# Stick-breaking attention: four steps under way, first steps in the single banks, values gathered into the last step's bank

## The chip, the cores and the metric

The kernel runs on one core of one Trainium2 chip. The metric is the time of one execution in microseconds (us); the median of three runs stands for the kernel. A core has five engines that run their own instruction lists in order and wait for each other through semaphores: TensorE (PE in the rows, with its weight loads as PEld), VectorE (DVE), ScalarE (ACT), GpSimd (POOL) and SyncE (SP, which here only starts transfers). TensorE writes its results into a memory of eight banks; DVE and ACT read them there.

## The reference

Two blocks of a network run one after the other on 512 positions of width 1024. The change lies in the second block's attention, which is all that has to be seen here:

```python
def stick_breaking_attention(q, k, v):
    # beta[t,s] = sigmoid(q_t.k_s / sqrt(Dh)), s < t
    # A[t,s]    = beta[t,s] * prod_{s<j<t} (1 - beta[t,j])
    # o_t       = sum_{s<t} A[t,s] v_s
    ...
        z = jnp.einsum("bqhd,bkhd->bhqk", qb, kb) * scale
        ...
        log_beta = jax.nn.log_sigmoid(z)
        log_one_minus = jnp.where(mask, jax.nn.log_sigmoid(-z), 0.0)
        tail = lax.cumsum(log_one_minus, axis=3, reverse=True) - log_one_minus
        weights = jnp.where(mask, jnp.exp(log_beta + tail), 0.0)
        outs.append(jnp.einsum("bhqk,bkhd->bqhd", weights, vb))
```

There are 8 heads of 64. Around it stand a projection to queries, keys, values and two gates, a causal convolution of 31 taps on the gated part with a layer norm, and an output projection of the attention and the convolution together.

## The kernel before

Everything but the attention is large products: each weight is split into a part in a reduced format and a remainder, and each product is three matmuls (`mm3`, lines 127 to 129). TensorE is the engine that the whole kernel is built around; the others prepare its operands and read its results.

**The stretch of the change.** The heads are taken two at a time: four pairs of heads, `hp` from 0 to 3. The two heads of a pair are `e` = 0 and 1. For a pair the 512 keys are cut into blocks of 128, and these are worked in three steps `n`: step 0 holds key blocks 2 and 3, step 1 block 1, step 2 block 0 (`STEPS`, line 765). A step is 384, 384 or 512 columns wide for each head (`WIDE`). Each step has two halves of work:

- `sticks(hp, n)`: TensorE forms the scores `z` (line 785, 6 or 12 matmuls, then line 790 for the mask). Then softplus is worked out: an absolute value (on ACT at line 794 for the first two pairs, on DVE at line 797 for the last two), exp and log on ACT (lines 799 and 800), `max(z, 0) +` on DVE (line 801), and a split into a high part (a cast on ACT, line 135) and a low part (a subtraction on DVE, line 136). These two parts are the step's block, `blk(hp, n)`.
- `breaks(hp, n)`: TensorE subtracts from `z`, in the same bank, the sums over later keys: with `negone` the blocks of the pair's earlier steps (line 814) and with `negtri` the step's own block (line 817). ACT then takes the exponent (line 819): these are the weights, `taken(hp, n)`. They wait for the step's own chain of six operations, and the matmuls of line 814 also for the blocks of the earlier steps.

After the three steps of a pair, `gather(hp)` multiplies the weights with the values (line 829) and ACT and DVE split the result into `qT` (lines 135 and 136, tile G).

**Banks.** The scores of a step lie in a double bank (`pair()`, tag pp, of which there are three). Two single banks (`ps0`, `ps1`) are left: `project()`, which forms the values before the attention, uses both in turn, `gather` takes `ps0`, and the norm of the convolution (`conv_norm`, line 889) `ps1`. A `pair` or a `single` is free again when its last reader is done.

**Order.** The code is written with the steps of `sticks` up to two ahead of `breaks` (line 979), and the first step of the next pair is not taken ahead while the last one of this pair is open. A scheduler then lays out each engine's list from the code by its own simulation, so the lists below are what counts. In these lists 120 convolution taps on DVE (line 851, tile H, 128x512 each) stand between the attention's operations, and ACT also splits weights for later products (lines 199 and 202). After the attention the same list goes on with `attended(u)`, the output projection of its result (lines 127 to 129 on tile G), parts of which stand already among the last pair's steps; then the same for the convolution's half.

Of the kernel before, what the change touches and what calls it, by code (L numbers as in the profile page):

```python
# [10 lines left out]
F32 = mybir.dt.float32  # L11
# [68 lines left out]
def block_kernel(  # L80
# [694 lines left out]
    def sticks(hp, n):  # L775

        w = WIDE[n]
        zt = pair()
        z = zt[:, :, :w]

        for i, (ks, qs) in enumerate(((kT[0], qT[0]), (kT[0], qT[1]), (kT[1], qT[0]))):
            for a in STEPS[n]:
                for e in range(2):
                    hs = slice(e * HD, (e + 1) * HD)
                    pe.matmul(z[:, e, cols_of(a)], ks[hs, hp, a * P : (a + 1) * P],  # L785
                              qs[hs, hp, a * P :], start=i == 0 and a < 3, stop=False,
                              skip_group_check=True)
        for a in STEPS[n]:
            for e in range(2):
                pe.matmul(z[:, e, cols_of(a)][:, :P], identr, never, start=False, stop=False,  # L790
                          skip_group_check=True)
        ex = v3(t4(), 2, w)
        if hp < 2:
            act.activation(ex, z, AF.Abs)
        else:

            dve.tensor_scalar(ex.bitcast(I32), z.bitcast(I32), 0x7FFFFFFF, None,
                              ALU.bitwise_and)
        act.activation(ex, ex, AF.Exp, scale=-1.0)
        act.activation(ex, ex, AF.Ln, bias=1.0)  # L800
        dve.scalar_tensor_tensor(ex, z, 0.0, ex, ALU.max, ALU.add)
        zs[hp, n] = z
        return copy_split(*blk(hp, n), ex)

    def breaks(hp, n):

        w = WIDE[n]
        z = zs.pop((hp, n))
        for e in range(2):
            for a in STEPS[n]:  # L810
                out = z[:, e, cols_of(a)]
# [7 lines left out]
        return act.activation(taken(hp, n), z, AF.Exp)  # L819

    def gather(hp):

        o = single(0)
# [40 lines left out]
    def place(i):  # L864
        if i not in stk:
            name = ("D0", "B0", "D1", "C0", "C1", "B1", "E1")[i]
            stk[i] = slot(name, F32R if i < 4 else F32)
        return stk[i]

    def blk(hp, n):  # L870

        tl = place((hp % 2, 2, 3)[n])
        return tuple(part(tl, 2, WIDE[n], 2 * WIDE[n] * i) for i in range(2))

    def taken(hp, n):

        at = (0, 1024 * (hp % 2), 768)[n]
        return part(place(6 if n == 1 else 4 + hp % 2), 2, WIDE[n], at)
# [94 lines left out]
    conv(10, sticks(*seq[0]))  # L973
    conv(14, sticks(*seq[1]))
    project()
    todo = 2
    for i, x in enumerate(seq):

        while todo < len(seq) and todo <= i + 2 and not (x[1] == 2 and seq[todo][1] == 1):
            conv(2, sticks(*seq[todo]))  # L980
            todo += 1
        weighted = breaks(*x)
        if x[1] == 2:
            gathered = gather(x[0])
# [131 lines left out]
```

## Time and profile before

| | |
|---|---|
| median of three runs | 1245.53 us (1244.40 to 1246.41) |
| the profiled execution | 1245.94 us |
| span of its instructions | 1244.2 us |
| TensorE busy | 1230.3 us, 99% of the span |
| VectorE, ScalarE busy | 754.0 us (61%), 495.0 us (40%) |
| TensorE's granted clock, mean | 0.995 |

The profile is of one execution; its own time lies 1.74 us above its span and 0.41 us above the median. [...] Times in the rows are microseconds from the span's start; the attention's steps lie between about 752 and 842 us.

### The profile page before, as it was taken

To read this page: it belongs to the slowest core of one execution; us is meant where nothing else is said; L and a number is where in the kernel's file an instruction comes from. 1 tells how busy PE (TensorE), PEld (TensorE's weight loads), DVE (VectorE), ACT (ScalarE), POOL (GpSimd) and SP (SyncE) were. 2 spreads that over 40 slices of the span, in tenths; PEclk is the share of its full clock that TensorE was granted. 3 is DMA by queue.
4 is the path that set the end of the run, shared out by engine and by line. 5 is a ranking of instruction groups with operands and counts; after the bars stand their busy time and mean duration, and the time that the engine had idled before them with its cause. 6 is when DMAs were issued, how large, how long until landed. Compare 5 with 4: busy or idle time off the path is not lost.

```text
span 1244.2 us, 13667 instructions
## 1 busy us (share of the span) xinstructions
PE 1230.3 (99%) x5712; PEld 1014.1 (82%) x5712; DVE 754.0 (61%) x823; ACT 495.0 (40%) x534; POOL 113.5 (9%) x137
## 2 busy tenths in 40 slices
PE   9999999999999999999999999999999999999998
PEld 7889888788888888888888887667888888888887
DVE  7855634744766674466373899877575555346532
ACT  6433424623544342243255338764343333123310
POOL 1100210012000000000053440000400000000000
PEclk9999999999999999999999999899999999999999
DMA  7223222312222222222346254301322222222222
GB/s 274 101 104 132 102 102 68 136 68 98 73 100 102 102 102 102 88 85 99 119 152 169 68 130 104 106 1 68 102 102 82 89 100 102 102 102 102 84 70 83
DMA packets 21597, 126.71 MB, mean 102 GB/s; under 512 B 2336, under 2 KB 4256, under 8 KB 7840
## 3 DMA queue, kind: packets, MB, share of 16 engines
q1 hardware_dynamic: 20096, 117.20, 26.7%
q0 software_dynamic: 1152, 8.39, 3.5%
q8 instruction: 44, 0.72, 0.2%
q10 hardware_dynamic: 288, 0.26, 0.1%
q14 instruction: 17, 0.14, 0.0%
HBM read 115.35 MB, written 2.10 MB: 94 GB/s over the span
## 4 chain that ended last, share of the span: by engine, by line
PE 90%; DVE 4%; POOL 2%; ACT 2%; issue 1%; DMA 1%; SPq 0%; DVEq 0%; POOLq 0%; ACTq 0%
PE pp L129 27%; PE pp L127 27%; PE pp L128 27%; DVE H L851 2%; PE ps L128 1%; PE ps L129 1%; PE ps L127 1%; POOL col L746 1%; PE pp L814 1%; PE pp L817 1%; PE ps L829 1%; DMA wlo<-raw 1%; POOL col L745 1%; PE pp L785 0%; PE ps L326 0%
## 5 line engine op out<-in xcount | busy, mean ns | idle before, releaser
L199 ACT CAST whi<-raw 128x2048 fp32r<-128x2048 f32 (+3 forms) x109 | 197.9, 1817 | 415.5 <-PE pp L128 335.7
L129 PE MATMUL pp<-B,wlo 128*128 128x512 f32 x672 | 262.5, 391 | 0.2
L127 PE MATMUL pp<-B,whi 128*128 128x512 f32 x672 | 261.7, 390 | 0.8 <-ACT whi L199 0.7
L128 PE MATMUL pp<-C,whi 128*128 128x512 f32 x672 | 262.2, 390 | 0.0
L205 DVE TENSOR_TENSOR wlo<-raw,whi 128x2048 fp32r<-128x2048 f32 (+3 forms) x101 | 219.3, 2172 | 66.1 <-ACT whi L199 65.6
L128 PE MATMUL pp<-G,whi 128*128 128x512 f32 x448 | 175.0, 391 | 0.0
L129 PE MATMUL pp<-F,wlo 128*128 128x512 f32 x416 | 162.2, 390 | 0.0
L127 PE MATMUL pp<-F,whi 128*128 128x512 f32 x416 | 161.5, 389 | 0.0
L129 PEld LDWEIGHTS pp<-B,wlo 128*128 128x128 f32 x672 | 126.1, 188 | 28.2 <-DVE wlo L205 1.5
L127 PEld LDWEIGHTS pp<-B,whi 128*128 128x128 f32 x672 | 126.3, 188 | 28.0 <-ACT whi L199 1.7
L128 PEld LDWEIGHTS pp<-C,whi 128*128 128x128 f32 x672 | 126.2, 188 | 26.8 <-issue 0.5
L128 PEld LDWEIGHTS pp<-G,whi 128*128 128x128 f32 x448 | 84.1, 188 | 17.5 <-issue 0.2
L655 DVE SCALAR_TENSOR_TENSOR H<-H,sm,H 128x512 f32<-128x512 f32 x132 | 92.8, 746 | 0.7
L634 DVE TENSOR_TENSOR A<-pp,A 128x1024 f32<-128x1024 f32 x23 | 28.2, 1224 | 105.5 <-PE pp L129 105.5
L129 PEld LDWEIGHTS pp<-F,wlo 128*128 128x128 f32 x416 | 78.1, 188 | 16.5 <-issue 0.2
L127 PEld LDWEIGHTS pp<-F,whi 128*128 128x128 f32 x416 | 78.1, 188 | 16.4 <-issue 0.2
L851 DVE SCALAR_TENSOR_TENSOR H<-H,sm,H 128x512 f32<-128x512 f32 x120 | 83.2, 742 | 2.7 <-ACT H L132 2.5
L660 DVE TENSOR_TENSOR H<-pp,rb 128x1024 f32<-128x1024 f32 x22 | 26.8, 1224 | 50.6 <-PE pp L129 44.4
L132 ACT ACTIVATE H<-H,sm 128x512 f32<-128x512 f32 x70 | 54.3, 808 | 4.6 <-DVE H L707 4.6
L1010 DVE TENSOR_TENSOR H<-pp,rb 128x512 f32<-128x512 f32 x22 | 15.2, 691 | 60.4 <-PE pp L129 55.3
L127 PE MATMUL pp<-D,whi 128*128 128x512 f32 x112 | 43.6, 389 | 0.0
L128 PE MATMUL pp<-E,whi 128*128 128x512 f32 x112 | 43.6, 389 | 0.0
(315 smaller groups left out, 1826.3 us busy)
## 6 DMA issues: line engine op xcount, KB each, us to landing
raw<-in_wts SPq DMA_DIRECT2D x99, 1024.0 KB, 4.8
wlo<-raw POOLq DMA_DIRECT2D x8, 1024.0 KB, 7.0
raw<-in_wts SPq DMA_DIRECT2D x8, 768.0 KB, 4.2
A<-in_xT SPq DMA_DIRECT2D x3, 512.0 KB, 6.7
out<-A SPq DMA_DIRECT2D x3, 512.0 KB, 2.8
D<-in_memT SPq DMA_DIRECT2D x1, 1024.0 KB, 11.4
raw<-in_wts SPq DMA_DIRECT2D x3, 256.0 KB, 7.6
A<-in_xT SPq DMA_DIRECT2D x2, 256.0 KB, 3.9
```

What stands on the lines that cost most here:

```text
L127: pe.matmul(out, wh, xh, start=start, stop=False, **kw)
L128: pe.matmul(out, wh, xl, start=False, stop=False, **kw)
L129: pe.matmul(out, wl, xh, start=False, stop=stop, **kw)
L132: act.activation(out, in_, AF.Identity, scale=scale, bias=bias)
L199: act.copy(hi[:, cs], raw[:, cs])
L205: dve.tensor_tensor(lo[:, cs], raw[:, cs], hi[:, cs].bitcast(F32), ALU.subtract)
L634: dve.tensor_tensor(hu, pt, hu, ALU.add)
L655: dve.scalar_tensor_tensor(dst, hs[:, k : k + 512], w(k), dst, ALU.mult, ALU.add)
L660: dve.tensor_tensor(hs[:, :, 2:], pt, over2(rb), ALU.mult)
L745: pool.tensor_scalar(ms, ms, rr2[:, t : t + 1], EPS, ALU.mult, ALU.add)
L851: tap = dve.scalar_tensor_tensor(cv[:, i, :], cc[:, i, k : k + 512], par("dw_w", 4 * k + i), cv[:, i, :], ALU.mult, ALU.add)
L1010: dve.tensor_tensor(hs[:, 2:514], pt[:, 0, :], rb, ALU.mult)
```

## The change

Three things are altered together.

- **Where the scores of a step lie.** Step 0 of every pair of heads now takes the two single banks, one for each head; steps 1 and 2 take a double bank as before. So three double banks and the two singles can hold four open steps. What reads or writes the scores of step 0 in one instruction over both heads (the absolute value, the max, the exponent) is two instructions of half the width.
- **The order.** `sticks` runs in the order of `pre`: (0,1), (0,2), (0,0), and then for each later pair steps 1, 0, 2. The first two are written before `project()`, which still uses the single banks; `breaks` keeps its order 0, 1, 2. Up to three steps are taken ahead of a `breaks`, and one more between a pair's last `breaks` and its `gather`.
- **The gather.** It writes into the first half of the double bank of the pair's own step 2 (`zs[hp, 2][0]`), after the exponent of that step has read it, and no longer into `ps0`.

The places of the blocks and the weights follow: step 1's block now has two places in turn (it had one), step 0's and step 2's as before two and one; the weights of steps 1 and 2 have one place each (they had two).

```diff
--- before.py
+++ after.py
@@ -775,40 +775,47 @@
     def sticks(hp, n):
 
         w = WIDE[n]
-        zt = pair()
-        z = zt[:, :, :w]
+
+        if n:
+            zt = pair()
+            z = [zt[:, e, :w] for e in range(2)]
+            zs[hp, n] = zt, z, [(slice(0, 2), zt[:, :, :w])]
+        else:
+            z = [single(e)[:, :w] for e in range(2)]
+            zs[hp, n] = None, z, [(e, z[e]) for e in range(2)]
+        whole_z = zs[hp, n][2]
 
         for i, (ks, qs) in enumerate(((kT[0], qT[0]), (kT[0], qT[1]), (kT[1], qT[0]))):
             for a in STEPS[n]:
                 for e in range(2):
                     hs = slice(e * HD, (e + 1) * HD)
-                    pe.matmul(z[:, e, cols_of(a)], ks[hs, hp, a * P : (a + 1) * P],
+                    pe.matmul(z[e][:, cols_of(a)], ks[hs, hp, a * P : (a + 1) * P],
                               qs[hs, hp, a * P :], start=i == 0 and a < 3, stop=False,
                               skip_group_check=True)
         for a in STEPS[n]:
             for e in range(2):
-                pe.matmul(z[:, e, cols_of(a)][:, :P], identr, never, start=False, stop=False,
+                pe.matmul(z[e][:, cols_of(a)][:, :P], identr, never, start=False, stop=False,
                           skip_group_check=True)
         ex = v3(t4(), 2, w)
-        if hp < 2:
-            act.activation(ex, z, AF.Abs)
-        else:
-
-            dve.tensor_scalar(ex.bitcast(I32), z.bitcast(I32), 0x7FFFFFFF, None,
-                              ALU.bitwise_and)
+        for e, ze in whole_z:
+            if hp < 2:
+                act.activation(ex[:, e], ze, AF.Abs)
+            else:
+
+                dve.tensor_scalar(ex[:, e].bitcast(I32), ze.bitcast(I32), 0x7FFFFFFF, None,
+                                  ALU.bitwise_and)
         act.activation(ex, ex, AF.Exp, scale=-1.0)
         act.activation(ex, ex, AF.Ln, bias=1.0)
-        dve.scalar_tensor_tensor(ex, z, 0.0, ex, ALU.max, ALU.add)
-        zs[hp, n] = z
+        for e, ze in whole_z:
+            dve.scalar_tensor_tensor(ex[:, e], ze, 0.0, ex[:, e], ALU.max, ALU.add)
         return copy_split(*blk(hp, n), ex)
 
     def breaks(hp, n):
 
-        w = WIDE[n]
-        z = zs.pop((hp, n))
+        _, z, whole_z = zs[hp, n]
         for e in range(2):
             for a in STEPS[n]:
-                out = z[:, e, cols_of(a)]
+                out = z[e][:, cols_of(a)]
                 for b in range(a + 1, 4):
                     for s in blk(hp, 0 if b > 1 else 1):
                         pe.matmul(out[:, (b - a) * P :], negone, s[:, e, cols_of(b)], start=False,
@@ -816,11 +823,14 @@
                 for i, s in enumerate(blk(hp, n)):
                     pe.matmul(out, negtri, s[:, e, cols_of(a)], start=False, stop=i == 1,
                               skip_group_check=True)
-        return act.activation(taken(hp, n), z, AF.Exp)
+        for e, ze in whole_z:
+            last = act.activation(taken(hp, n)[:, e], ze, AF.Exp)
+        return last
 
     def gather(hp):
 
-        o = single(0)
+
+        o = zs[hp, 2][0][:, 0, :]
         for n in range(3):
             for a in reversed(STEPS[n]):
                 for e in range(2):
@@ -863,19 +873,19 @@
 
     def place(i):
         if i not in stk:
-            name = ("D0", "B0", "D1", "C0", "C1", "B1", "E1")[i]
-            stk[i] = slot(name, F32R if i < 4 else F32)
+            name = ("C0", "B0", "D1", "B1", "D0", "C1", "E1")[i]
+            stk[i] = slot(name, F32R if i < 5 else F32)
         return stk[i]
 
     def blk(hp, n):
 
-        tl = place((hp % 2, 2, 3)[n])
+        tl = place((hp % 2, 2 + hp % 2, 4)[n])
         return tuple(part(tl, 2, WIDE[n], 2 * WIDE[n] * i) for i in range(2))
 
     def taken(hp, n):
 
-        at = (0, 1024 * (hp % 2), 768)[n]
-        return part(place(6 if n == 1 else 4 + hp % 2), 2, WIDE[n], at)
+        i, at = ((5 + hp % 2, 0), (6, 768), (5, 768))[n]
+        return part(place(i), 2, WIDE[n], at)
 
     cl = None
     ch = []
@@ -970,17 +980,22 @@
 
     seq = [(hp, n) for hp in range(4) for n in range(3)]
 
-    conv(10, sticks(*seq[0]))
-    conv(14, sticks(*seq[1]))
+    pre = [(0, 1), (0, 2), (0, 0)] + [(hp, n) for hp in range(1, 4) for n in (1, 0, 2)]
+
+    conv(10, sticks(*pre[0]))
+    conv(14, sticks(*pre[1]))
     project()
     todo = 2
     for i, x in enumerate(seq):
-
-        while todo < len(seq) and todo <= i + 2 and not (x[1] == 2 and seq[todo][1] == 1):
-            conv(2, sticks(*seq[todo]))
+        while todo < len(pre) and todo <= i + (3 if x[1] < 2 else 2):
+            conv(2, sticks(*pre[todo]))
             todo += 1
         weighted = breaks(*x)
         if x[1] == 2:
+
+            if todo < len(pre):
+                conv(2, sticks(*pre[todo]))
+                todo += 1
             gathered = gather(x[0])
     with tc.issue_after(weighted.ins):
         act.preload_act_table_set("silu_and_others")
```

The lists of three engines show what the scheduler made of it. Tile names in them carry a number; C, B and D with a number are blocks, E and C the weights, t a step's work tile, H the convolution, G the attention's result. In the list of before, `D_5066` is the block of (0,0) and `D_5093` that of (0,1).

TensorE where `project()` ends, before: after the last product of the values (lines 128 and 129) stand the first matmuls of `breaks(0, 0)`.

```order
L128 MATMUL ps_5202<-wlo,B_4163 128x512
L129 MATMUL ps_5202<-whi,C_4165 128x512
L814 MATMUL pp<-D_5066,negone 128x128 x2
L817 MATMUL pp<-D_5066,negtri 128x256 x2
L817 MATMUL pp<-D_5066,negtri 128x128 x2
```

The same place now (`ps_5221` and `ps_5220` are the two single banks of step (0,0), `C_5245` its block, `D_5058` the block of (0,1)):

```order
L797 MATMUL ps_5221<-never,identr 128x128 x2
L821 MATMUL pp<-D_5058,negone 128x384 x2
L792 MATMUL ps_5220<-G_4552,F_4797 128x256
L792 MATMUL ps_5220<-G_4552,F_4797 128x128
L792 MATMUL ps_5220<-G_4553,F_4797 128x256
L792 MATMUL ps_5220<-G_4553,F_4797 128x128
L792 MATMUL ps_5220<-G_4552,F_4798 128x256
L792 MATMUL ps_5220<-G_4552,F_4798 128x128
L797 MATMUL ps_5220<-never,identr 128x128 x2
L821 MATMUL ps_5220<-C_5245,negone 128x128
L821 MATMUL ps_5221<-C_5245,negone 128x128
```

The scores of (0,0) were made inside `project()`; now they are made after it, and the first matmul that needs their block follows at once.

VectorE in the same stretch, before (`t_5237` is the work tile of (0,2), `t_5278` that of (1,0)):

```order
L801 SCALAR_TENSOR_TENSOR t_5237<-pp,t_5237 128x1024
L851 SCALAR_TENSOR_TENSOR H_2138<-H_2137,sm,H_2138 128x512 x9
L136 TENSOR_TENSOR C_5242<-t_5237,C_5242 128x1024
L851 SCALAR_TENSOR_TENSOR H_2138<-H_2137,sm,H_2138 128x512 x13
L801 SCALAR_TENSOR_TENSOR t_5278<-pp,t_5278 128x768
```

And now (`t_5238` is the work tile of (0,0), `t_5259` that of (1,1)):

```order
L136 TENSOR_TENSOR D_5085<-t_5080,D_5085 128x1024
L861 SCALAR_TENSOR_TENSOR H_2138<-H_2137,sm,H_2138 128x512 x23
L810 SCALAR_TENSOR_TENSOR t_5238<-ps_5220,t_5238 128x384
L810 SCALAR_TENSOR_TENSOR t_5238<-ps_5221,t_5238 128x384
L810 SCALAR_TENSOR_TENSOR t_5259<-pp,t_5259 128x768
L136 TENSOR_TENSOR C_5245<-t_5238,C_5245 128x768
```

The operation behind the long run of taps belonged to pair 1; now it is (0,0)'s own.

ScalarE around the exponent of (1,2), the last step of the second pair, before (line 819 into `B_5378`, 1024 wide):

```order
L799 ACTIVATE t_5397<-t_5397 128x768
L819 ACTIVATE E_5300<-pp 128x768
L800 ACTIVATE t_5397<-t_5397 128x768
L819 ACTIVATE B_5378<-pp 128x1024
L135 CAST D_5066<-t_5397 128x768
```

And now (line 827 into `C_5281`):

```order
L827 ACTIVATE E_5326<-pp 128x768
L807 ACTIVATE t_5382<-t_5382 128x768
L808 ACTIVATE t_5382<-t_5382 128x768
L807 ACTIVATE t_5423<-t_5423 128x768
L808 ACTIVATE t_5423<-t_5423 128x768
L135 CAST D_5058<-t_5382 128x768
L135 CAST C_5245<-t_5423 128x768
L827 ACTIVATE C_5281<-pp 128x1024
```

Between the exponents of (1,1) and (1,2) stood one operation of the next pair; now six operations of two of its steps, the casts among them, stand there.

## Rows read from the trace of the kernel before

Idle time before an instruction and what ended it stand in square brackets where the view gives them.

**Rows 1.** The page: busy time of each engine; TensorE's granted clock in 40 slices.

```profile
PE 1230.3 (99%) x5712; PEld 1014.1 (82%) x5712; DVE 754.0 (61%) x823; ACT 495.0 (40%) x534; POOL 113.5 (9%) x137
...
PEclk9999999999999999999999999899999999999999
```

**Rows 2.** Windows: length, then busy PE, PEld, DVE, ACT, POOL; clock, DMA share, GB/s.

```profile
772.58:784.80 12.22, 12.22 (x84) 8.79 (x82) 12.22 (x19) 11.00 (x11) 1.18 (x2) 1.00 0.95 186
784.80:804.96 20.16, 18.05 (x95) 13.33 (x93) 14.54 (x19) 12.78 (x16) 0.00 (x0) 0.75 0.24 97
804.96:826.16 21.20, 17.58 (x124) 12.27 (x122) 17.34 (x22) 14.12 (x19) 0.00 (x0) 1.00 0.00 1
826.16:841.76 15.60, 15.60 (x80) 11.85 (x78) 8.56 (x12) 8.72 (x10) 0.66 (x1) 1.00 0.00 1
841.76:857.36 15.60, 14.95 (x65) 11.66 (x63) 15.19 (x19) 7.44 (x11) 0.38 (x1) 1.00 0.06 15
```

**Rows 3.** Waits of TensorE from 740 to 880: total, times, longest.

```profile
PE ps L829 <- ACT C L819: 1.5, 1, 1.5
...
PE pp L127 <- DVE A L957: 0.7, 1, 0.7
```

**Rows 4.** Half-microsecond windows, columns as in group 2.

```profile
788.50:789.00 0.50, 0.50 (x6) 0.50 (x6) 0.50 (x2) 0.50 (x2) 0.00 (x0) 1.00 1.00 426
...
799.00:799.50 0.50, 0.50 (x3) 0.50 (x3) 0.00 (x0) 0.50 (x1) 0.00 (x0) 0.50 0.00 0
799.50:800.00 0.50, 0.50 (x3) 0.42 (x3) 0.00 (x0) 0.50 (x2) 0.00 (x0) 0.99 0.00 0
```

**Rows 5.** TensorE's instructions: start, duration, then the operation.

```profile
772.58 0.33 PE L814 MATMUL pp<-D,negone 128*128 128x128 f32 x2
...
790.38 1.12 PE L814 MATMUL pp<-B,negone 128*128 128x256 f32 x4 [0.86 <-DVE t L801]
791.43 1.54 PE L785 MATMUL pp<-G,F 64*128 64x256 f32 x12
...
808.55 0.91 PE L785 MATMUL pp<-G,F 64*128 64x256 f32 x12 [0.90 <-ACT C L819]
809.39 0.66 PE L790 MATMUL pp<-never,identr 128*128 128x128 f32 x4
...
816.09 0.97 PE L814 MATMUL pp<-D,negone 128*128 128x384 f32 x6
...
820.54 1.08 PE L829 MATMUL ps<-C,E 128*64 128x512 f32 x4 [1.55 <-ACT C L819]
```

**Rows 6.** VectorE's instructions, the same view.

```profile
753.95 6.83 DVE L851 SCALAR_TENSOR_TENSOR H<-H,sm,H 128x512 f32<-128x512 f32 x10
760.70 0.94 DVE L801 SCALAR_TENSOR_TENSOR t<-pp,t 128x768 f32<-128x768 f32 x1
...
768.14 1.21 DVE L801 SCALAR_TENSOR_TENSOR t<-pp,t 128x1024 f32<-128x1024 f32 x1
769.27 6.03 DVE L851 SCALAR_TENSOR_TENSOR H<-H,sm,H 128x512 f32<-128x512 f32 x9
...
776.37 8.69 DVE L851 SCALAR_TENSOR_TENSOR H<-H,sm,H 128x512 f32<-128x512 f32 x13
784.99 0.94 DVE L801 SCALAR_TENSOR_TENSOR t<-pp,t 128x768 f32<-128x768 f32 x1
```

**Rows 7.** ScalarE's instructions, the same view.

```profile
754.92 1.52 ACT L794 ACTIVATE t<-pp 128x768 f32<-128x768 f32 x2
756.32 1.58 ACT L799 ACTIVATE t<-t 128x768 f32<-128x768 f32 x2
...
763.00 1.01 ACT L794 ACTIVATE t<-pp 128x1024 f32<-128x1024 f32 x1
...
773.45 1.04 ACT L135 CAST C<-t 128x1024 fp32r<-128x1024 f32 x1
...
776.21 0.66 ACT L132 ACTIVATE E<-ps,rr 128x512 f32<-128x512 f32 x1
776.78 1.89 ACT L199 CAST whi<-raw 128x2048 fp32r<-128x2048 f32 x1
```

## Prediction

> **What bounds the kernel now.** I read the page first: TensorE is busy for 1230.3 of 1244.2 us [rows 1], so only its stops, its clock and its amount of work can move the time. The amount does not change: every matmul of before is still there with its shape. So I look for the place where TensorE is not served. The 40 slices show the granted clock below full in one slice alone, and that is the attention. The windows cut this stretch at its landmarks [rows 2]. From 772.58 to 784.80, right behind the values, TensorE is busy without a gap, and so is DVE. From 784.80 to 826.16 TensorE is idle for 20.16 - 18.05 = 2.1 and 21.20 - 17.58 = 3.6 us, 5.7 us together, in waits such as that of the gather for an exponent [rows 3]. The second of these windows also has a mean clock of 0.75. [...] Before the fall TensorE had waited several times for its operands; after it, it worked from 790.38 to the rise, 9.1 us, without a stop [rows 5]. The same scores of a step 0 start at 791.43 with 1.54 us for their twelve matmuls at half clock, and with 0.91 at full. So half of the 9.1 us, 4.6 us, is lost to the clock. What a deeper run-ahead can win here is 5.7 + 4.6, and 0.7 for one wait behind the attention [rows 3]: 11.0 us at the very most.
>
> **The change part by part, against the profiled execution's 1245.94 us.**
>
> *A stop at the start.* This is what the lists show and the diff does not. Before, three steps were made inside the projection of the values, and (0,0) had its block ready when that ended: at 772.58 the first matmul of breaks starts at once [rows 5]. Now (0,0) needs the single banks, which the projection holds to its end. Its scores come behind it, and next in TensorE's list stands breaks of the same step, which needs the whole chain of six operations. TensorE's list is run in order, so everything that was prepared, and the scores of (1,0) too, is queued behind that wait.
>
> How long is it? The projection ends some 0.4 us earlier, since the three steps made inside it are now (0,1), (0,2) and (1,1) with 18 score matmuls and not 24: about 772.2. DVE: I count its list from the run of taps at 753.95 [rows 6]. Before, 38 taps, three max-adds and three subtractions stand up to the operation at 784.99, with no gap in the last 12 us [rows 2]. Now 36 taps, two and two stand ahead of the max-add of (0,0). A tap is 8.69/13 = 0.67 us, and a 768-wide operation starts the next one about 0.9 after itself (0.94 long): 784.99 - 1.3 - 1.8 = 781.9. ACT: the weight splits and the last evacuation of the values come first; the cast that stood among them at 773.45 (1.04 long) is gone, so the split at 776.78 ends near 777.6. Then the list has two half-wide absolute values of (0,0), one of (1,1), two exps and the log: five times about 0.74 [rows 7], 781.3. The two engines agree, and the max-adds run 781.9 to 782.9, the cast to 783.7, the subtraction (behind the max-add of (1,1)) to 784.7. TensorE has in all that time the scores of (0,0), some 1.4 us (0.91 and 0.66 less their overlap [rows 5]), and four matmuls with the earlier block and the high part, 0.7 us by the six-matmul group of 0.97. 784.7 - 772.2 - 2.1 = 10.4 us. I take **+10.0**, with ends 9 and 11.
>
> *The clock.* TensorE stands almost still from 773 to 784, longer than what brought the clock down before, so it falls. The nearest row for its return is 9.1 us of work [rows 4, 5]. That is the loss of before once more, 4.6 us, only earlier. **0**, with ends -3 (it returns in a third of that) and +4.6 (it falls once more later).
>
> *Later stops.* Three places in the lists still wait, and I walked them with the prices of the rows: on ACT about 0.74 for 768 wide and 1.0 for 1024 [rows 7], on DVE 0.9 and 1.2 [rows 6]. First, breaks of (1,0): behind its scores ACT has two half absolute values, exp, the exponent of (0,2), log, and then two 1024-wide operations of (1,2), all ahead of its cast, 5.9 us, and the subtraction 0.9. TensorE has 5.2 us meanwhile (the second half of a step-2 breaks 1.45, the scores of (1,2) 1.2, a gather 2.6): 1.6 us of stop. Second, the gather of pair 1. It now writes into the bank that the exponent of (1,2) reads, and needs that exponent's output too, and this stands behind the casts of (2,1) and (2,0) in ACT's list. Those wait for DVE: 1.9 for three absolute values, 1.5 for the last exp and log on ACT, 1.0 for two max-adds, 0.8 for a cast, 1.0 for the exponent, 6.2 us against 4.1 of TensorE's work (breaks and scores of a step 2): 2.1. Third, the gather of pair 2 with the same pattern: 2.1. Together 5.8 us, as much as the 5.7 of before. My prices leave out what TensorE loses between groups of different kinds, which fills part of a stop, so I take 4.0: 4.0 - 5.7 = **-1.7**, with ends -5.7 (no stop is left) and +2.5.
>
> *Splits.* Step 0 has its readers of the scores twice at half the width: 12 more instructions, six on ACT and six on DVE. Two absolute values of 768 in a row end after 1.52, one of 1024 takes 1.01 [rows 7]; the second of the pair thus adds 0.71, which is 0.92 ns a column against 0.99. The width carries nearly all of it, so a split costs 0 to 0.1, and three or four lie on the chains above: 0.2, inside the terms already taken. [...]
>
> *The tail.* The 0.7 wait behind the attention goes, since the convolution's chain there is ordered otherwise; the convolution's first low part stands on DVE behind more of `attended` and comes up to 1.5 late. **+0.8**, ends -0.7 and +1.5. The second place of step 1's block and the single places of the weights of steps 1 and 2 cost nothing that I can find: those weights' exponents come after the previous gather in the lists anyway.
>
> Sum: 10.0 + 0 - 1.7 + 0.8 = +9.1 us. 1245.94 + 9.1 = 1255.0 for the profiled execution, which lies 0.4 above the median: **1254.5**.
>
> **The rivals.**
>
> *The later pairs run without stops and the clock returns early.* For it: after the start, four steps are under way, and the waits of before are of just the kind that this removes. Against it: the exponents behind casts in ACT's list. 10.0 - 3 - 5.7 + 0.8 = +2.1: 1247.6. From 2.5 us down this is the same time as before.
>
> *Faster: the stop is no more than the chain itself.* If the chain of (0,0) began when its scores are there (774) and nothing stood ahead of it, it would be two half absolute values, exp and log 2.2, max-adds 1.0, cast 0.8, subtraction 0.9: 779. The stop would be 4.9, short enough that the clock might hold (-4.6), and with the later stops down to 2 (-3.7) it gives 4.9 - 4.6 - 3.7 + 0.8 = -2.6: 1242.9. It decides for faster as soon as the stop stays under about 7 us. Against it: ACT's splits and DVE's 23 taps do stand ahead in the lists, and both engines are full in that window [rows 2].
>
> *A second fall of the clock.* A stop of 2 us at a gather, in a stretch of small matmuls, could bring it down again; before, a wait of 1.5 us at 820.54 [rows 3, 5] did not. +9.1 + 4.6: 1259.1.
>
> *The change does not do what it says*, that is, no more steps are under way. The lists say otherwise: scores of four steps stand ahead of the first breaks. But that is also its cost. No chance of its own.
>
> **How the numbers follow.** Forecast (1250 to 1258) 0.67; second fall 0.11; stops vanish and early clock 0.14; faster 0.08. The range reaches from the second rival's time to just over the second fall's: 1248 to 1260, which leaves out the faster case, part of the one about 1247.6, and a little above. What a measurement can tell from no change is some 0.2%, 2.5 us: 1243.0 to 1248.0. Faster by more than that: 0.07, the case of 1242.9 with what lies around it. Within: 0.11, most of the one at 1247.6. Slower: 0.82.
>
> **What would show it.** In the profile of after TensorE should stand idle for about 7 us up to some 784, waiting for ACT's cast of C, with DVE on taps until about 782; the clock should read 0.50 in the window after; the end of the last gather should come some 8 to 10 us later than 841.76. Waits of a gather for the exponent into C (line 827) near 2 us, twice, would confirm the later stops. If the first stop is under 7 us, or the clock never falls, I am wrong on the sign.

## The result: 1261.6 us, 1.3% slower, and where the time went

| | before | after |
|---|---|---|
| median | 1245.34 us (4 runs) | 1261.64 us (4 runs, 1257.22 to 1263.96) |
| ratio | | 1.0129, 95% interval 1.0099 to 1.0158 |
| profiled execution, span | 1245.94, 1244.2 us | 1259.43, 1257.7 us |
| TensorE's mean granted clock | 0.995 | 0.991 |

The prediction was 1254.5 us with a range of 1248 to 1260: the direction was right and the time lies 1.6 us above the range. The four executions of after spread over 6.7 us, and those with the lower mean clock are the longer ones (0.992, 0.991, 0.986, 0.986 for 1257.22, 1259.43, 1263.85, 1263.96).

The page of after, against [rows 1]: the amount of work is the same (5712 matmuls, six instructions more on VectorE and on ScalarE), and now two slices of the clock are below full.

```profile
PE 1234.1 (98%) x5712; PEld 1018.8 (81%) x5712; DVE 755.9 (60%) x829; ACT 496.1 (39%) x540; POOL 113.1 (9%) x137
...
PEclk9999999999999999999999998899999999999999
```

TensorE's waits between 740 and 900 us (total, times, longest), against [rows 3]: the gather's wait for an exponent is still there (line 839, twice), and casts into tile C (line 135) have come in front of all: the first step's, 7.45 us, and one of pair 2, 1.66 us.

```profile
PE ps L821 <- ACT C L135: 9.1, 2, 7.5
PE ps L792 <- ACT E L132: 1.6, 1, 1.6
PE pp L839 <- ACT C L827: 1.4, 2, 1.1
PE pp L128 <- DVE H L136: 1.3, 1, 1.3
PE ps L821 <- ACT B L135: 1.1, 1, 1.1
PE ps L821 <- DVE B L136: 0.4, 1, 0.4
```

TensorE's instructions at these waits (start, duration, operation; the wait and what ended it in brackets), against [rows 5]:

```profile
771.84 0.90 PE L792 MATMUL ps<-G,F 64*128 64x256 f32 x6
...
775.14 0.90 PE L792 MATMUL ps<-G,F 64*128 64x256 f32 x6 [1.64 <-ACT E L132]
...
783.86 0.69 PE L821 MATMUL ps<-C,negone 128*128 128x128 f32 x2 [7.45 <-ACT C L135]
...
798.74 0.44 PE L821 MATMUL ps<-B,negone 128*128 128x128 f32 x2 [1.08 <-ACT B L135]
...
813.25 0.44 PE L821 MATMUL ps<-C,negone 128*128 128x128 f32 x2 [1.66 <-ACT C L135]
...
831.34 0.87 PE L839 MATMUL pp<-C,E 128*64 128x128 f32 x8 [1.11 <-ACT C L827]
```

VectorE and ScalarE ahead of the long stop, against [rows 6, 7]. The 23 taps run to 781.9 without a gap; ScalarE's second log ended at 781.3 and its cast then waited 1.70 us for the max-add behind the taps.

```profile
766.63 15.33 DVE L861 SCALAR_TENSOR_TENSOR H<-H,sm,H 128x512 f32<-128x512 f32 x23
781.86 1.02 DVE L810 SCALAR_TENSOR_TENSOR t<-ps,t 128x384 f32<-128x384 f32 x2
```

```profile
779.69 1.59 ACT L808 ACTIVATE t<-t 128x768 f32<-128x768 f32 x2
782.98 0.83 ACT L135 CAST C<-t 128x768 fp32r<-128x768 f32 x1 [1.70 <-DVE t L810]
```

The windows cut at the stops (length, busy PE, PEld, DVE, ACT, POOL; clock, DMA share, GB/s), against [rows 2]:

```profile
771.84:783.86 12.02, 2.93 (x19) 2.32 (x19) 11.93 (x20) 10.32 (x13) 1.08 (x2) 0.69 0.96 186
783.86:797.66 13.80, 13.76 (x78) 10.96 (x78) 5.49 (x8) 7.57 (x11) 0.00 (x0) 0.77 0.37 144
797.66:818.00 20.34, 16.90 (x92) 12.55 (x91) 16.04 (x21) 12.11 (x16) 0.00 (x0) 0.83 0.00 0
818.00:828.00 10.00, 10.00 (x60) 7.94 (x58) 7.13 (x9) 7.87 (x11) 0.00 (x0) 0.83 0.01 2
828.00:853.20 25.20, 24.09 (x129) 16.96 (x127) 13.30 (x18) 11.84 (x16) 0.00 (x0) 1.00 0.00 1
```

In half-microsecond windows the clock reads 0.50 in four stretches: 776.5 to 790.1, 800.4 to 803.8, 814.1 to 817.5 and 824.3 to 827.7. Before there was one, 789.2 to 799.5 [rows 4]. The last of the four lies inside the row 818.00:828.00, where TensorE is busy for 10.00 of 10.00 us. Windows at the last three falls, and at the last rise (length, busy PE; clock, DMA share, GB/s):

```profile
800.00:800.50 0.50, 0.50 (x6) 0.90 0.00 0
...
814.00:814.50 0.50, 0.33 (x4) 0.55 0.00 0
...
823.50:824.00 0.50, 0.50 (x6) 1.00 0.00 0
824.00:824.50 0.50, 0.50 (x5) 0.79 0.00 0
...
827.50:828.00 0.50, 0.50 (x3) 0.80 0.00 0
```

**One sum for every kernel of this study.** Take from the span TensorE's waits between 740 and 900 us, and the time lost at half clock (busy time times one minus the clock, over half-microsecond windows from 770 to 860). What is left lies between 1231.2 and 1235.7 us each time, so that differences of more than some 4 us between two profiled executions can be put down to one or the other, and smaller ones cannot:

| profiled execution | span | waits | half clock | rest |
|---|---|---|---|---|
| before | 1244.2 | 6.5 | 4.7 | 1233.0 |
| after | 1257.7 | 14.9 | 8.2 | 1234.6 |
| e1 first pair in a double bank | 1248.6 | 8.8 | 6.3 | 1233.5 |
| e2 gather alone | 1245.6 | 6.3 | 8.1 | 1231.2 |
| e3 filler (8.2 of it taken off too) | 1264.0 | 7.9 | 14.8 | 1233.1 |
| e4 taps behind | 1264.3 | 15.4 | 15.6 | 1233.3 |
| e5 taps and splits behind | 1252.3 | 12.9 | 4.7 | 1234.7 |
| e6 e1, splits behind | 1251.9 | 11.9 | 7.1 | 1232.9 |
| e7 e1, two ahead | 1247.6 | 6.4 | 6.8 | 1234.4 |
| e8 halves alone | 1244.2 | 5.7 | 4.9 | 1233.6 |
| e9 no chain | 1237.8 | 2.8 | 0.0 | 1235.0 |
| e10 e1, exponent first | 1248.8 | 10.3 | 5.1 | 1233.4 |
| e11 pairs 1 to 3 free | 1254.2 | 11.3 | 10.7 | 1232.2 |
| e12 pair 0 free | 1250.5 | 10.9 | 3.9 | 1235.7 |

Between before and after that is +8.4 of waits, +3.5 of clock and +1.6 of rest, together the 13.5 us of the two profiled executions. Of the rest, 1.1 lies ahead of the attention (TensorE is idle for 3.6 us of the first 740 before, 4.7 after), where the change moves nothing.

### The profile page after: what moved, and what is told of

It is laid out like the page before. It is cut to its first block, busy times and chain, and to the rows that moved or that the text cites. A ratio compares the mean times of both kernels' runs of the same rounds, so it can differ in the third digit from the quotient of the medians.

```text
span 1257.7 us, 13680 instructions
## 1 busy us (share of the span) xinstructions
PE 1234.1 (98%) x5712; PEld 1018.8 (81%) x5712; DVE 755.9 (60%) x829; ACT 496.1 (39%) x540; POOL 113.1 (9%) x137
## 4 chain that ended last, share of the span: by engine, by line
PE 89%; DVE 6%; POOL 2%; ACT 2%; issue 1%; DMA 0%; SPq 0%; DVEq 0%; POOLq 0%; ACTq 0%
PE pp L129 27%; PE pp L128 27%; PE pp L127 27%; DVE H L861 4%; POOL col L746 1%; PE ps L127 1%; PE ps L129 1%; PE ps L128 1%; PE pp L821 1%; PE pp L839 1%; PE pp L824 1%; POOL col L745 1%; PE ps L326 0%; DMA A<-in_xT 0%; PE ps L824 0%
## 5 line engine op out<-in xcount | busy, mean ns | idle before, releaser
L129 PEld LDWEIGHTS pp<-F,wlo 128*128 128x128 f32 x416 | 78.1, 188 | 16.3 <-issue 0.2
L129 PE MATMUL pp<-D,wlo 128*128 128x512 f32 x112 | 43.6, 390 | 0.0
## 6 DMA issues: line engine op xcount, KB each, us to landing
D<-in_memT SPq DMA_DIRECT2D x1, 1024.0 KB, 10.9
```

The lines of the kernel that those rows point to most:

```text
L129: pe.matmul(out, wl, xh, start=False, stop=stop, **kw)
```

## The experiments

Each time stands beside the kernel before on the same chip. The changed kernel ("after") lay 16.3 us above before where it was run, and what an experiment takes off is reckoned from there.

**e1: is it the stop at the start?** The first pair's step 0 gets a double bank and is made inside the projection, as before. Pair 1 then takes its steps in the order 0, 1, 2; pairs 2 and 3 stay as in after.

```diff
-        if n:
+        if n or not hp:
             zt = pair()
...
-    pre = [(0, 1), (0, 2), (0, 0)] + [(hp, n) for hp in range(1, 4) for n in (1, 0, 2)]
+    pre = [(0, 0), (0, 1), (0, 2), (1, 0), (1, 1), (1, 2)]
+    pre += [(hp, n) for hp in range(2, 4) for n in (1, 0, 2)]
```

> Undoes one part of the change: the first pair's step 0 lies in a double bank again and its scores are made inside the projection of the values; the later pairs keep the single banks, the split readers, four open steps and the gather in the last step's bank. Theory A (the price is the stop at the start, 7.45 us up to 783.86 and 1.64 before it, with the 3.1 us that the clock costs behind it): TensorE goes straight from the values into the first breaks, and the time falls by 10 to 13 us from that of the changed kernel, to 1246 to 1251 us. Rival B (the price lies in the later pairs, in the casts ahead of the exponents and the falls of the clock there): it stays above 1255 us, with no stop at 776 to 784 all the same.

1248.46 us against 1245.57, ratio 1.0027 [1.0015, 1.0039]. That is 2.9 us above before, so 13.4 of the 16.3 us are gone with this stop. Its waits show what is left, and why it still does not win: other casts and exponents now come last.

```profile
PE ps L821 <- ACT B L135: 4.2, 2, 3.3
PE pp L839 <- ACT C L827: 2.4, 1, 2.4
PE pp L128 <- DVE H L136: 1.3, 1, 1.3
PE ps L821 <- DVE B L136: 0.9, 1, 0.9
```

**e2: the gather's bank alone.** Before, with the gather in the bank of the pair's step 2.

```diff
-        zs[hp, n] = z
+        zs[hp, n] = zt, z
...
-        o = single(0)
+        o = zs[hp, 2][0][:, 0, :]
```

> The kernel before with one part of the change alone: the gather writes into the bank of the pair's own step 2. Theory A: the gather needs that step's exponent for its last matmuls anyway, so all it loses is the head start of its first eight matmuls: 0 to +2 us, 1245 to 1247.5. Rival (this part is what costs): each of four gathers waits some 2 us more, +6 to +8 us, above 1251.

1247.54 against 1245.57, ratio 1.0017 [1.0008, 1.0027]: 2.0 us. With three double banks and no single one for the gather, the next scores wait for it (first row), which before they never did.

```profile
PE pp L785 <- DVE G L136: 1.8, 1, 1.8
PE pp L785 <- ACT E L819: 1.7, 1, 1.7
```

**e3: keep TensorE busy in the stop.** After, with 14 and 56 spare 128x128 matmuls behind the scores of (0,0).

```diff
...
+        if (hp, n) == (0, 0):
+            spare = zs[0, 1][0][:, 0, 384:512]
+            for e, count in ((1, 14), (0, 56)):
+                with tc.issue_after(masks[e].ins):
+                    for _ in range(count):
+                        pe.matmul(spare, negone, negone, start=False, stop=False,
+                                  skip_group_check=True)
```

> The changed kernel with 70 matmuls of 128x128 more, inside the two stops behind the projection, into columns that nothing reads (14 in the first, 56 in the second). They should take about as long as the stops, so that TensorE's next real matmul starts at about 784 as before. Theory A (behind the stop 3.1 us go to the half clock): the clock reads 1.00 through 784 to 790 and the time falls by 2 to 4 us, to 1257 to 1260. Rival (the half clock hides behind waits that come anyway): 0. If the small matmuls are not what holds the clock, it reads 0.50 as before and the matmuls themselves run late by some us.

1263.72 against 1245.57: no gain over after. The clock stayed at 1.00 to 783.9, through the filler and the 1.21 us that it left open, and fell just as the work behind began. In this execution more was lost behind 800 than in after (14.8 us in all). The four executions run from 1258.42 us (mean clock 0.996) to 1265.85 (0.988), so what the filler does to the later falls stays open.

```profile
776.30 6.42 PE L805 MATMUL pp<-negone 128*128 128x128 f32 x56
783.93 0.69 PE L829 MATMUL ps<-C,negone 128*128 128x128 f32 x2 [1.21 <-ACT C L135]
```

**e4 and e5: what stands ahead of the chain.** e4 is after with the 14 taps of `conv(14, ...)` written behind (0,0).

```diff
-    conv(14, sticks(*pre[1]))
+    conv(0, sticks(*pre[1]))
     project()
-    todo = 2
+    conv(16, sticks(*pre[2]))
+    todo = 3
```

> The changed kernel with the 14 convolution taps that followed (0,2) now following (0,0), so that DVE's run ahead of the max of (0,0) is 9 and not 23. Theory A (ScalarE's list ends at about the same time, its log of (0,0) at 780.5): the stop ends 1.3 us earlier, near 782.5, and the time is 0 to 2 us less than that of the changed kernel. Rival (DVE's taps alone make the stop): it ends near 779, and the time is 5 us less or more than 5.

1259.33 against 1245.57: 2.5 less than after, which does not stand clear of the spread (1258.15 to 1267.01 here, 1257.22 to 1263.96 in after). In the trace the longest stop is 6.2 and not 7.45 us, since ScalarE's queue is last then.

e5 is e4 with two weight splits taken out of ScalarE's list there.

```diff
-        ws = [weights() for _ in range(2)]
+        while len(state["ready"]) < 2:
+            prep()
+        ws = [state["ready"].pop(0) for _ in range(2)]
         weighted = breaks(*x)
+        if i in (3, 6):
+            with tc.issue_after(weighted.ins):
+                prep()
```

> The changed kernel with everything taken out of the way of the first step's chain: the 14 taps that stood ahead of it on VectorE come behind it (as in e4), and the two weight splits (four instructions of 1.9 us on ScalarE) that stood ahead of it are made later, one behind the exponent of step (1,0), one behind that of (2,0). Theory A (the stop at the start is the queue in front of a six-operation chain): the evacuation of the values now ends near 773.6, the second single bank's scores follow without their wait of 1.6, and absolute values, exps, logs, max-adds, cast end near 779.8 instead of 783.9, so 4.0 us less: 1257.6. If a stop of 5 us instead of 10 also holds the clock there, another 3: 1254.5. This is what the prediction's faster rival assumed (a stop of no more than the chain itself) and it would still be slower than the kernel before. Rival B (the time is set by the falls of the clock in the later score and break matmuls and not by the stop): the stop shrinks but the clock falls as often, and the time stays above 1259. Rival C (the splits are late for the products behind the attention): a new wait of 1 to 3 us on whi or wlo at lines 127 to 129.

1254.19 against 1245.16, ratio 1.0081 [1.0065, 1.0098]: 7.3 us less than after. TensorE starts on (0,0) at 780.23 and not at 783.86; the wait of 1.64 for the second single bank is gone too. So 3.6 us are the queue's.

```profile
780.23 0.69 PE L821 MATMUL ps<-C,negone 128*128 128x128 f32 x2 [5.45 <-ACT C L135]
```

Most of the 5.45 us that remain is the chain itself, but not all: on ScalarE the absolute value of (1,1) (128x768, line 802) and one of the two exps (line 807) still run ahead of the log of (0,0), some 1.4 us.

```profile
775.20 0.80 ACT L802 ACTIVATE t<-pp 128x768 f32<-128x768 f32 x1
775.89 1.57 ACT L807 ACTIVATE t<-t 128x768 f32<-128x768 f32 x2
777.36 1.57 ACT L808 ACTIVATE t<-t 128x768 f32<-128x768 f32 x2
```

The profiled executions lie 5.4 us apart: 3.6 less at this stop, 1.6 more at later ones, and 3.5 less for the clock (4.7 us at half clock and not 8.2). The faster rival of the prediction put the decision at a stop under about 7 us. That is built here, the clock fell all the same (3.0 us lost at this stop, 1.7 later), and the kernel is 9.0 us slower than before. An order without the 1.4 us, or with other work of TensorE in the stop, was not run.

**e6 and e10: can e1 be made to win?** e6 is e1 with the splits moved as in e5. e10 moves them behind other exponents and writes the next pair's step 0 behind the exponent that the gather waits for; its lines against e6:

```diff
-        while todo < len(pre) and todo <= i + (3 if x[1] < 2 else 2):
+        while todo < len(pre) and todo <= i + 3 - x[1]:
...
-        if i in (3, 6):
+        if i in (4, 7):
...
-                conv(2, sticks(*pre[todo]))
+                with tc.issue_after(weighted.ins):
+                    chain = sticks(*pre[todo])
+                conv(2, chain)
```

> e1 (first pair's step 0 in a double bank, made inside the projection) with the two weight splits behind the exponents of (1,0) and (2,0). In e1 the second single bank came free only behind ScalarE's splits (evacuation at 776.3), the scores of (1,0) for the second head came at 779.5 and TensorE waited 3.3 us for the cast of that step at 788.8. Theory A: with the splits away VectorE's run of 11 taps is the last (to about 783), max-adds and cast end near 785, where TensorE is done with the gather: the 3.3 goes, 1248.5 - 3.3 = 1245.2, no difference from before. If the clock then does not fall either, another 2 to 3 us: 1242.5, faster than before. Rival: the wait moves to the next place in ScalarE's list (the splits now stand before casts of pair 2): 1248.

> e1 with two changes to ScalarE's list: the two weight splits come behind the exponents of (1,1) and (2,1) (e6 put them behind (1,0) and (2,0), where the cast of (2,1) had to wait 5.2 us), and the step 0 of a later pair is written behind the last exponent of the pair before it, so that no exp of the next pair stands ahead of the exponent that a gather waits for; step 0 of the next pair is thus one place later. Theory A: the 3.3 us stop of e1 for the first cast of pair 1 shrinks to 1.7 as in e6, the 2.4 us wait of the gather for its exponent to under 1; 1248.5 - 1.6 - 1.5 = 1245.4, and up to 3 less where the clock then falls once and not twice: 1242.5, faster than before. Rival: the step that is now later makes the next breaks wait for its block instead, 2 to 3 us: 1248.

1253.41 against 1245.16 and 1250.83 against 1245.32: both worse than e1. The stop of 3.3 us at pair 1 goes as expected, and a longer one opens at pair 2, for the cast of (2,0) (e6's wait, then e10's):

```profile
PE ps L821 <- ACT D L135: 5.2, 1, 5.2
```

```profile
PE ps L821 <- ACT D L135: 3.5, 1, 3.5
```

The rivals were right that the wait moves on, and too low on the time (1248 for both). e6's windows up to that wait and across it:

```profile
772.00:796.90 24.90, 23.95 (x162) 18.63 (x161) 24.24 (x35) 18.84 (x23) 0.86 (x1) 1.00 0.13 27
796.90:802.28 5.38, 0.15 (x3) 0.01 (x1) 3.88 (x7) 4.87 (x7) 0.00 (x0) 0.78 0.64 151
```

TensorE now works 23.95 of the first 24.90 us, at full clock, and has used up what was prepared. VectorE was busy for 24.24 of them, with taps among the rest, and so the block of (2,0) comes 5.2 us later than TensorE wants it. It is VectorE's list and not, as e6's rival had it, the splits on ScalarE: ScalarE waits for VectorE's absolute value for 2.77 us up to 796.92. The stop has moved on by one pair.

**e7: is the fourth step worth anything?** e1 with the run-ahead of before.

```diff
-        while todo < len(pre) and todo <= i + (3 if x[1] < 2 else 2):
+        while todo < len(pre) and todo <= i + 2:
...
-            if todo < len(pre):
-                conv(2, sticks(*pre[todo]))
-                todo += 1
```

> e1 with the run-ahead of the kernel before: steps at most two ahead of a breaks, none between a pair's last breaks and its gather. So the fourth open step is gone, while the single banks for step 0 and the gather in step 2's bank stay. If running four steps ahead is worth something, this is slower than e1 by up to the 5 us of stops that four steps should hide: 1250 to 1253. If the fourth step brings nothing, because the casts and exponents behind each other in ScalarE's list set the stops: 1248.5, as e1. If the fourth step itself brings stops (casts of two later steps ahead of an exponent): 1246 to 1247.

1249.74 against 1245.16, ratio 1.0037 [1.0024, 1.0050]. e1 has 1.0027 [1.0015, 1.0039]: the fourth step may bring 1.2 us, but the intervals overlap.

**e8: the halves alone.** Before, with the readers of step 0's scores in two instructions of half the width.

```diff
-            act.activation(ex, z, AF.Abs)
+        parts = (0, 1) if n == 0 else (slice(0, 2),)
+        for e in parts:
...
+                act.activation(ex[:, e], z[:, e], AF.Abs)
...
```

> The kernel before with one part of the change: what reads or writes the scores of step 0 over both heads (absolute value, max-add, exponent) is two instructions of half the width, 12 more instructions in all; banks and order stay. The prediction took 0.2 us. [...] Expected 1245.5 to 1246.0, no difference that can be measured; over 1247 would mean that the halves delay the chains by more than any row showed.

1246.77 against 1245.16, ratio 1.0012 [1.0004, 1.0021]: 1.6 us [0.5, 2.6], not 0.2, and above what was expected of the run. The profiled execution, 0.7 us below the median, does not tell where: its waits (5.7 us) and its clock (4.9) are about those of before.

Nor is the cause shown: in the trace of after, two halves back to back take hardly longer than one whole instruction (0.87 and 0.82 us):

```profile
776.78 0.87 ACT L802 ACTIVATE t<-ps 128x384 f32<-128x384 f32 x2
777.53 0.82 ACT L802 ACTIVATE t<-pp 128x768 f32<-128x768 f32 x1
```

What e1 keeps above before, 2.9 us, is no more than the gather's bank (e2, 2.0) and the halves (e8, 1.6) cost by themselves. So beside the stop at the start these two can account for what the change costs (a sum of single runs), and nothing here shows a gain from the fourth open step.

**e9: no stops at all.** After with all its instructions, but TensorE reads the keys in place of the blocks and weights, so that it never waits for the chain; the attention's result is not computed.

```diff
-                    for s in blk(hp, 0 if b > 1 else 1):
+                    for s in kT:
...
-                for i, s in enumerate(blk(hp, n)):
+                for i, s in enumerate(kT):
...
-            dve.scalar_tensor_tensor(ex[:, e], ze, 0.0, ex[:, e], ALU.max, ALU.add)
+            dve.scalar_tensor_tensor(ex[:, e], ex[:, e], 0.0, ex[:, e], ALU.max, ALU.add)
...
-            last = act.activation(taken(hp, n)[:, e], ze, AF.Exp)
+            last = act.activation(taken(hp, n)[:, e], ze, AF.Abs)
...
-                    pe.matmul(o[hs, a * P :], v2[:, a, vs], taken(hp, n)[:, e, cols_of(a)],
+                    pe.matmul(o[hs, a * P :], v2[:, a, vs], kT[0].bitcast(F32)[:, e, cols_of(a)],
```

> The changed kernel with the softplus chain taken out of TensorE's way: the matmuls of breaks read the keys (kT) and not the step's blocks, the gather reads the keys and not the weights, the max-add reads its own tile and not the scores, and the exponent is an absolute value of the same shape. All instructions stay, in number and size; the attention's result is not computed. TensorE then waits only for banks. The spans so far agree with one sum: 1233 to 1235 us, and the waits of TensorE, and the time lost at half clock (work at half clock, times a half). Theory A (stops bring the falls of the clock): without stops the clock stays full, about 1234 + 2 of waits + 1.7 outside the span = 1237. Rival B (the attention's own matmuls, 64 rows or 128 to 384 columns, bring the clock down whether TensorE waits or not): falls stay, 4 to 8 us lost, 1241 to 1245.

1239.98 against 1245.32, ratio 0.9961 [0.9949, 0.9974]. With matmuls of the same shapes and no stop the clock stays full through the whole attention:

```profile
773.50:800.00 26.50, 26.50 (x183) 20.42 (x182) 22.59 (x34) 24.55 (x33) 1.13 (x2) 1.00 0.63 159
800.00:831.00 31.00, 30.91 (x178) 22.81 (x176) 26.54 (x36) 21.67 (x29) 0.00 (x0) 1.00 0.00 1
```

So the matmuls' small sizes alone did not bring the clock down; without stops there was no fall (1.00 in both windows). (The operands hold other values too, which no run separates.) The time is 5.3 us below before and 3 above theory A's 1237: by the sum e9 has 8.4 us less of waits and half clock than before, and a rest that is 2.0 higher.

**e11 and e12: which stops bring which falls?** The edit of e9 for pairs 1 to 3 alone (`kT if hp else ...`), and for pair 0 alone (`kT if not hp else ...`).

> The changed kernel with the edit of e9 for pairs 1 to 3 alone (breaks and gather read the keys, the max-add its own tile, the exponent is an absolute value): the stop at the start for (0,0) stays, shortened by 1 to 2 us because the breaks of (1,1) can fill it; the later stops go. Their result is not computed. The question is what brings the falls of the clock behind 795 in the changed kernel (three, some 5 us in the profiled execution). Theory A (each later stop brings its own fall): the clock is full from about 790 on, one stretch at half behind the first stop, 3 us; 1261.6 - 4.5 (later stops) - 5 to 7 (later falls) - 1.5 = 1249 to 1251. Rival B (the long first stop upsets the clock for the rest of the attention): falls remain behind 795, 1254 to 1257.

> The mirror of e11: the edit of e9 for pair 0 alone, whose result is not computed, pairs 1 to 3 as in the changed kernel. The stop at the start is gone and with it its half-clock stretch, the later stops stay. Theory A (later stops bring the later falls): still one to three half-clock stretches behind 790, 3 to 7 us; 1240.0 of e9 and some 5 of later stops and 3 to 7 of clock: 1248 to 1252. Rival B (only the long first stop brings falls): clock full, 1244 to 1246, as fast as before.

e11: 1254.74 against 1246.07. The time is the one that rival B gave, but its windows speak for theory A: from the rise of the clock (791.9) to 846.6 there is no stop, and no half clock either. It is slow again by a stop that was not meant, 5.7 us at the convolution's norm, with a half-clock stretch of its own. And its first half-clock stretch costs 6.8 us (774.8 to 791.9), where theory A had 3, although the waits there are only 1.64, 1.28 and 1.94 us.

```profile
774.60:791.60 17.00, 13.44 (x51) 11.92 (x52) 13.44 (x20) 10.02 (x14) 0.85 (x1) 0.50 0.82 216
791.60:849.40 57.80, 55.00 (x336) 40.54 (x336) 44.26 (x57) 37.55 (x50) 0.00 (x0) 1.00 0.00 1
849.40:860.00 10.60, 7.73 (x22) 6.48 (x23) 3.96 (x7) 0.00 (x0) 1.03 (x1) 0.52 0.28 99
```

e12: 1252.06 against 1246.07, within theory A's range. The stop at the start only moved to pair 1 (5.93 us up to 794.87, for a max-add behind the taps). Its one half-clock stretch, 788.2 to 801.9, began 0.7 us ahead of that stop and 1.9 us behind one of 0.68. Later stops of 0.75 and 0.39, and of 0.86 and 0.87, brought no fall in this execution (one of the other four took 1258.85 us at a mean clock of 0.986). So e12 does not decide on the later stops; it shows that pairs of stops under 0.9 us can pass without one.

```profile
786.33 0.90 PE L792 MATMUL ps<-G,F 64*128 64x256 f32 x6 [0.68 <-ACT C L828]
...
794.87 1.01 PE L822 MATMUL pp<-B,negone 128*128 128x384 f32 x2 [5.93 <-DVE t L811]
...
810.23 0.44 PE L822 MATMUL ps<-C,negone 128*128 128x128 f32 x2 [0.75 <-ACT C L135]
```

No kernel of the study that computes the whole beats the kernel before.

## Why the prediction was right on the sign and short on the size

Against the profiled execution, by the prediction's own terms. It was put at 1255.0 us and took 1259.43, 4.4 more; the terms below give -0.9, +3.5, +0.5 and -0.2, and the rest of the sum above +1.6, which makes it up to within 0.1.

- **The stop at the start: right.** The max-adds were put at 781.9 and start at 781.86, the cast was to end at 783.7 and ends at 783.81. TensorE stands for 9.1 us in two waits (1.64 and 7.45), where 10.4 was worked out and 10.0 taken, with ends 9 and 11. Of the 1.3 too much, 0.8 is the subtraction, which I had on the path: the first matmuls on C start as the cast ends, and VectorE subtracts beside them. The work of TensorE in between is 0.8 longer (2.93 us and not 2.1), and the projection ended 0.4 earlier than taken (771.84).
- **The clock, taken as 0 with ends of -3 and +4.6: this step failed.** It rested on one row, the 9.1 us of work until the clock came back [rows 4, 5], and on the 1.5 us wait at 820.54 that brought no fall. The first half was pessimistic: behind the stop the clock came back after 6.3 us of work, and this stretch cost 3.1 us. But three more falls followed, each worth about 1.7 us. The profiled execution lost 8.2 and not 4.7, +3.5 where 0 was taken.
- **From the profiled execution to the median, -0.4 taken: wrong as well.** Two of the four executions had a still lower mean clock (0.986), and the median lies 2.2 above the profiled one. If that is the clock's too, which the mean clocks suggest and no trace shows, the clock's term was some +5.7 for the median, above its own upper end.
- **Later stops, -1.7: nearly right in sum, with some luck in the places.** Three places were named, with 1.6, 2.1 and 2.1; they measure 1.47 (1.08 + 0.39), 1.98 (1.66 + 0.32) and 1.11, together 4.6 where 4.0 was taken, against 5.8 before. At the second place the gather itself waits for 0.32 us only: the 1.66 stand at matmuls of (2,0) ahead of it, for the cast that the gather's exponent is queued behind. The sign of two gathers that wait near 2 us each did not come.
- **Splits, 0.2 inside the terms: too small.** e8 measures 1.6 [0.5, 2.6] for them alone. The rest of the sum is 1.6 higher in after, but 1.1 of it lies ahead of the attention.
- **The tail, +0.8: right.** 1.28 us for the low part on VectorE in place of 0.7: +0.6.

The rival "a second fall of the clock" gave 1259.1 for the median, which is 1259.6 for the profiled execution, and that took 1259.43. It named what then came, further falls of the clock, but the near hit is partly luck: one further fall of 4.6 us was priced, and three of 1.7 came, behind an earlier return. Its chance of 0.11 was too low: one wait that had brought no fall was read as evidence that such waits bring none. Before, two shorter stops already stood ahead of its one fall at 789.2, and one of 0.86 came right behind it:

```profile
787.00 0.33 PE L814 MATMUL pp<-B,negone 128*128 128x128 f32 x1 [0.59 <-ACT B L135]
787.99 0.33 PE L814 MATMUL pp<-B,negone 128*128 128x128 f32 x1 [0.66 <-DVE B L136]
```

With several stops ahead, more than one fall had to be allowed for, and the range had to reach to two or three. The faster rival's main condition, a stop under 7 us, is met by e5, which takes 1254.2; its other one, later stops down to 2 us, is not met there. The rival of the later pairs without stops failed on its condition: 4.6 us of later stops stayed, though the clock did return early.

Two questions stay open. What decides when the clock falls: in after it fell at 824.3, ten microseconds behind the last stop, in e12 1.9 us behind one of 0.68, in e12 again not at all behind two pairs of stops of that size, and in before not behind one of 1.55. And where the 1.6 us of the halves lie.

## What to carry to other kernels

A deeper run-ahead is paid for by the step that loses its place in the cover: look in the lists for the first step that is no longer prepared, count what stands ahead of its chain on every engine, and then ask what remains when most of it is cleared away (here 5.5 us). Where TensorE stands still several times in a short stretch, let the range hold more than one fall of the clock: here three came behind 795 in after, and none behind the two pairs of stops under 0.9 us in e12. Subtracting waits and half-clock time from the span gave the same rest within 2.3 us up or down in fourteen kernels; where two differ by clearly more than that, it tells whether the slower one waits more or runs at a lower clock.

## What the runs showed of the hardware

- The clock can fall behind a stop and not in it, as at 824.3 in after, amid 10 us of work without a gap; without any stop (e9) matmuls of the same shapes ran at 1.00 from 773.5 to 831.
- While small matmuls filled the stop the clock stayed at 1.00 (e3, to 783.9; without them it fell at 776.5), but it fell at the end of the 1.21 us that they left open, and the median was no lower than that of after.
- The same kernel runs at a different mean clock from one execution to the next: after 1257.22 us at 0.992 and 1263.96 at 0.986, e4 1258.15 at 0.992 and 1267.01 at 0.985. A profiled execution shows one of them, and the longer ones are those at the lower clock.
- Splitting twelve instructions into two of half the width each cost 1.6 us [0.5, 2.6] in all (e8), though two halves back to back take only 0.05 us longer than one whole in the trace (0.87 and 0.82).
